# Three idle products ahead of the second small turn, two adaLN tiles summed on VectorE, x's last turns ahead of the sums

## The chip, the core and the metric

The kernel runs on one core of a Trainium2 chip. The core has four engines that compute, each with its own queue, worked off in order: TensorE (PE in the profile; PEld is its loading of weights, which overlaps its products), VectorE (DVE), ScalarE (ACT) and GpSimd (POOL). SyncE (SP) issues transfers between the device's memory (HBM) and the core's own memory. Products are written to PSUM banks, from which DVE and ACT read. The metric is the device time of one execution in microseconds (us), the median of several runs.

## The reference

One layer, float32, on x of 256 tokens by 2048:

```python
h = rmsnorm(x, norm_g)                                   # (256, 2048)
mod = silu(c) @ ada_w + ada_b                            # (1, 3 * 2048)
shift, scale, gate = split(mod, 3)
h = h * (1.0 + scale) + shift
b_gate, c_gate, v, g = split(h @ sc_w_in, 4)             # sc_w_in: 2048 x 4 * 4096
u = causal_depthwise_conv(c_gate * v, conv_w)            # width 3
y = (b_gate * u * silu(g)) @ sc_w_out                    # sc_w_out: 4096 x 2048
out = rmsnorm(x + gate * y, final_g)
```

The large work is two products, h @ sc_w_in and y @ sc_w_out. adaLN's vector-matrix product, silu(c) @ ada_w, reads a matrix of 2048 x 6144.

## The kernel before, in words

Every large product is made of three products in a shorter float format: each operand is split into a rounded part (`hi`) and the remainder (`lo`), and hi\*hi, hi\*lo and lo\*hi are added up. `hi` of a weight tile is made by ACT (`split_hi`, L314), `lo` by DVE (`split_lo`, L319). The transposed and modulated h is split in the same way into the two halves of `hT` (`modulate`, L293).

The model dimension 2048 is cut into 16 blocks `k` of 128 rows. h's block k can be used as soon as adaLN's shift and scale for it are there. adaLN is therefore made in groups of two blocks: the group's columns of ada_w come in as tiles `at`, and the sum over the 16 row blocks, each times its value of silu(c), is built up. For all groups but the first DVE does that alone, on a tile `gv` (`ada_sums`, L420), and four transposes and a `reduce_sum` (`ada_done`, L429) end it. The products h @ sc_w_in start with the blocks that are ready and come back later for the rest: a part (`part`, L469) is one chunk of 512 output columns of one of the four quarters, over the blocks k0 to k1. In the first stage every part covers the first two blocks alone, so it needs one half tile of weights (128 x 1024, `raw_s`), or `raw0` for the very first part; later parts work on whole tiles (128 x 2048). A part's PSUM bank is copied out by ACT (`acc`, L465), added by DVE (L467), or refilled from `acc` ahead of the next products (L477). `plan` (L52) decides the order of parts and adaLN pieces from constants for costs.

Two kinds of order follow one another. From L181 to L379 the instructions are pinned: each engine runs them in the order in which the program writes them (`in_order`). This is the front, which the change touches. Behind it a scheduler orders the instructions of each engine, from its own estimate of time and from priorities; `behind(ended)` keeps chosen ones behind the front's last instruction of their engine. So an edit of the front can also move instructions behind it.

The front, engine by engine:

- SP issues the four pieces of x, twelve pieces of ada_w (`first_ada`, six tiles: rows k = 0 to 3, 4 to 7, 8 to 11, 12 and 13, 14, 15), the two pieces of raw0, and then the transfers behind the front. ACT issues the three small vectors c, norm_g and ada_b.
- PE makes the first small turn (c, L242), the second small turn (norm_g and ada_b, `tp_v`, L245), the idle products (`idle`, L248, whose results nobody reads), the turns of x (`turn_x`, L277, four groups of eight transposes, each group a bank `tp_x` of four blocks), and its share of the first adaLN group's sums (`sum0`, L348).
- The rows k in `ON_PE` are summed on PE, where silu(c), broadcast, is the moving operand and all sums add up in one bank, `sums0`. The other rows are summed on DVE in `gv0`; at the end PE adds `gv0` to the same bank, in two halves (L373). Row k = 15 is divided: its shift half goes to PE, its scale half to DVE.
- DVE squares the second half of the tokens of x, copies the second turn's result to `vec`, makes `rstd`, then runs the sums in gv0, the remainder of raw0's first block (L375), the sum with the bias (`mod`, L297), and the scalings and remainders of h (L301, L304).
- ACT makes silu(c), squares the first half of the tokens, scales the four pieces of x by rstd (L344), copies the turned x to `xs` with the norm's weight (`keep_x`, L286), rounds raw0's two blocks, and makes the rounded part of hT (L300).

A bank for `tp_x` is one of three (tag "mm"), which the parts behind the front use too, so the fourth group waits until ACT has emptied the first. The small turns, the idle products and `sums0` share two banks with the tag "sm".

Of the kernel before, what the change touches and what calls it, by code (L numbers as in the profile page):

```python
# [117 lines left out]
def short_conv_layer(ctx: ExitStack, tc: tile.TileContext, x, c, norm_g, ada_w, ada_b, w_in, conv_w, w_out, final_g, out):  # L118
# [17 lines left out]
    def slot(shape, name, dtype=F32):  # L136
        return slots.tile(shape, dtype, tag="slot", name=name)
# [48 lines left out]
    HX = D // 2  # L186
    GIVE = 300
    LEAD = 80
    IDLE = 6
    ON_PE = (3, 7, 10, 11, 13, 15)  # L190
    xt = [[slot([P, HX], f"x{t}{dh}") for dh in range(2)] for t in range(TT)]
    nc.scalar.dma_start(rows1[64:80, :], c.rearrange("o (k p) -> (o k) p", p=P))
    for t in range(TT):
# [33 lines left out]
    def turn(rows, lo, n, dst):  # L227
        tp = psum.tile([P, 512], F32, tag="sm", name="tp_v", bufs=2)[:, : n - lo]
        nc.tensor.transpose(tp, rows[lo:n, :], ident[lo:n, lo:n])
        if dst is not None:  # L230
            nc.vector.tensor_copy(dst, tp)
        return tp


    def idle(n):
        for _ in range(n):
            nc.tensor.matmul(tp_idle, ident, ones[:, 0:1].to_broadcast([P, 512]), start=True, stop=True)
# [4 lines left out]
    silu = nc.scalar.activation(silu_c, turn(rows1, 64, 80, None), AF.Silu)  # L242
    root = nc.scalar.activation(warm, eps_t, AF.Sqrt)
    tc.add_manual_dep(root.ins, silu.ins.name, after, reason="one change of table")
    tp_v = turn(rows1, 0, 64, None)  # L245
    gT = vec[:, 0:KT]
    bias = vec[:, KT : 3 * KT].rearrange("p (s k) -> p s k", s=2)
    idle(IDLE)  # L248


    ssq = const.tile([P, 2, TT], F32, tag="ssq", name="ssq")
# [25 lines left out]
    def turn_x(j):  # L277

        tp = psum.tile([P, CT, T], F32, tag="mm", name="tp_x")
        for i in range(CT):  # L280
            for t in range(TT):
                c0 = (j * CT + i) % 8 * P
                nc.tensor.transpose(tp[:, i, t * P : (t + 1) * P], xt[t][j // 2][:, c0 : c0 + P], ident)
        return tp

    def keep_x(j, tp):  # L286
        for i in range(CT):
            k = j * CT + i
            nc.scalar.activation(xs[j][:, i], tp[:, i], AF.Copy, scale=gT[:, k : k + 1])
# [3 lines left out]
    def modulate(k0, nk, sums):  # L293

        ks = slice(k0, k0 + nk)
        sums = sums.rearrange("p (s k) -> p s k", s=2)
        nc.vector.tensor_tensor(out=mod[:, :, ks], in0=sums, in1=bias[:, :, ks], op=ALU.add)  # L297
        for k in range(k0, k0 + nk):
            hf = xs[k // CT][:, k % CT, :]
            nc.scalar.activation(hh_[:, k], hf, AF.Identity, bias=mod[:, 0, k : k + 1], scale=mod[:, 1, k : k + 1])  # L300
            nc.vector.tensor_scalar(  # L301
                out=hf, in0=hf, scalar1=mod[:, 1, k : k + 1], scalar2=mod[:, 0, k : k + 1], op0=ALU.mult, op1=ALU.add
            )
            nc.vector.tensor_tensor(out=hl_[:, k], in0=hf, in1=hh_[:, k].bitcast(F32), op=ALU.subtract)  # L304
# [43 lines left out]
    def sum0(k, rows, col, halves=(0, 1)):  # L348


        for o in range(2 * NK0):
            if o // NK0 in halves:
                nc.tensor.matmul(
                    sums0[:, o * P : (o + 1) * P], rows[:, o // NK0, (o % NK0) * P : (o % NK0 + 1) * P],
                    col.to_broadcast([P, P]),
                    start=k == ON_PE[0] and o == 0, stop=k is None, skip_group_check=True,
                )

    for k in range(KT):
        c_k = silu_c[:, k : k + 1]  # L360
        at, gv = first_ada[k], gv0
        if k in ON_PE:
            if k == 10:
                keep_x(2, turn_x(2))
            sum0(k, at, c_k, (0,) if k == KT - 1 else (0, 1))
            if k < KT - 1:
                continue
            at, gv = at[:, 1], gv0[:, 1]
        if k == 0:
            nc.vector.tensor_scalar_mul(gv, at, c_k)  # L370
        else:
            nc.vector.scalar_tensor_tensor(out=gv, in0=at, scalar=c_k, in1=gv, op0=ALU.mult, op1=ALU.add)
# [2 lines left out]
    pieces0 = [split(raw0[:, 0 : CT * P], CT * P)]  # L375
    hi0 = [split_hi(raw0[:, k * CT * P : (k + 1) * CT * P], CT * P) for k in range(1, NK0)]
    modulate(0, NK0, sums0.rearrange("p (o f) -> p o f", o=2 * NK0)[:, :, 0])
    tp_3 = turn_x(3)
    pinned.close()  # L379
    with behind(ended):  # L380
        keep_x(3, tp_3)
# [350 lines left out]
```

## Time and profile before

| | us |
|---|---|
| median of 3 runs | 913.6 |
| lowest and highest run | 913.55, 913.6 |
| span of the profiled execution | 911.9 |
| PE busy | 895.7 |
| DVE busy | 616.2 |
| ACT busy | 464.6 |

The span goes from the first to the last profiled instruction; a run's time also holds what lies around it. A row of a timeline gives start, duration, engine, line, operation, the tiles written and read, their shapes, the count of instructions merged, and in brackets the idle time of the engine before it with what ended it. A row of the chain of waits gives start, duration and what was waited for. A row of the transfers' view gives the count, the size and the time from issue to landing. Matmuls overlap, so a row's busy time is a little longer than the distance to the next.

### The profile page before, as it was taken

The page shows a single profiled execution, that of the slowest core. Times are in us where ns is not written, and L with a number is a line of the kernel's source. Part 1 is how long each engine was busy: PE and PEld are TensorE (multiplying, and loading weights), DVE is VectorE, ACT ScalarE, POOL GpSimd, SP SyncE. Part 2 cuts the span into 40 slices and gives each one's busy share as a digit, 9 for nine tenths or more (in the row PEclk, how much of TensorE's full clock was granted, in tenths as well). Part 3 has the DMA queues.
Part 4 walks back from the last instruction along what each step waited for, and adds up shares of the span by engine and source line. Part 5 has one row for each costly group of instructions (what it writes and reads, how often), then busy time and mean ns, then how long its engine had stood idle before and what let it go on. Part 6 is the DMA issues. An engine that isn't in the chain of part 4 may idle for free.

```text
span 911.9 us, 16239 instructions
## 1 busy us (share of the span) xinstructions
PE 895.7 (98%) x7047; PEld 858.5 (94%) x7047; DVE 616.2 (68%) x593; ACT 464.6 (51%) x413; POOL 0.7 (0%) x6
## 2 busy tenths in 40 slices
PE   6999999999999999999999999999999999999996
PEld 4999999999999999999999999999999988888885
DVE  4889999989888899765545555545554544555882
ACT  6768856665558756743334433444333333443333
POOL 0000000000000000000000000000000000000000
PEclk9999999999999999999999999999999999999998
DMA  9999999999998698676656665566656486655542
GB/s 309 367 371 353 365 325 351 356 369 352 338 328 275 197 359 301 201 246 197 186 188 197 200 201 186 187 195 200 200 188 188 140 331 231 203 201 186 185 139 92
DMA packets 163752, 227.65 MB, mean 250 GB/s; under 512 B 5680, under 2 KB 104160, under 8 KB 163296
## 3 DMA queue, kind: packets, MB, share of 16 engines
q1 hardware_dynamic: 163552, 226.56, 74.8%
q8 instruction: 55, 0.90, 0.4%
q14 instruction: 17, 0.14, 0.0%
q10 hardware_dynamic: 128, 0.04, 0.0%
HBM read 224.49 MB, written 2.10 MB: 248 GB/s over the span
## 4 chain that ended last, share of the span: by engine, by line
PE 94%; DMA 3%; ACT 1%; SPq 1%; DVE 0%; issue 0%; ACTq 0%
PE mm_b L444 38%; PE mm_s L444 36%; PE mm_o L631 6%; PE mm_o L629 6%; PE mm_o L630 6%; DMA raw_s<-in_sc_w_in_dram 2%; DMA at<-in_ada_w_dram 1%; SPq L210 1%; DMA x<-in_x_dram 1%; ACT hi L314 0%; PE ps_gate L568 0%; PE tp_g L434 0%; ACT acc L465 0%; DVE lo L319 0%; ACT hT L300 0%; SPq L413 0%
## 5 line engine op out<-in xcount | busy, mean ns | idle before, releaser
L444 PE MATMUL mm_s<-hT,hi 128*128 128x256 f32 x2048 | 350.5, 277 | 0.2
L444 PE MATMUL mm_b<-hT,hi 128*128 128x256 f32 x2048 | 348.8, 276 | 0.0
L444 PEld LDWEIGHTS mm_s<-hT,hi 128*128 128x128 f32 x2048 | 308.7, 188 | 1.1 <-ACT hT L300 0.4
L444 PEld LDWEIGHTS mm_b<-hT,hi 128*128 128x128 f32 x2048 | 308.7, 188 | 0.2 <-issue 0.2
L444 PE MATMUL mm_b<-hT,lo 128*128 128x256 f32 x1024 | 282.6, 276 | 0.0
L444 PE MATMUL mm_s<-hT,lo 128*128 128x256 f32 x1024 | 282.2, 277 | 0.2 <-DVE lo L319 0.2
L319 DVE TENSOR_TENSOR lo<-raw,hi 128x2048 fp32r<-128x2048 f32 (+1 forms) x66 | 148.0, 2244 | 136.8 <-ACT hi L314 136.8
L314 ACT CAST hi<-raw 128x2048 fp32r<-128x2048 f32 (+1 forms) x66 | 123.7, 1874 | 200.2 <-PE mm_b L444 156.1
L444 PEld LDWEIGHTS mm_b<-hT,lo 128*128 128x128 f32 x1024 | 192.2, 188 | 0.2 <-issue 0.2
L444 PEld LDWEIGHTS mm_s<-hT,lo 128*128 128x128 f32 x1024 | 191.7, 188 | 0.7 <-DVE lo L319 0.6
L319 DVE TENSOR_TENSOR lo<-raw_s,hi 128x2048 fp32r<-128x2048 f32 (+1 forms) x80 | 147.6, 1850 | 25.6 <-ACT hi L314 24.6
L314 ACT CAST hi<-raw_s 128x2048 fp32r<-128x2048 f32 (+1 forms) x80 | 124.2, 1559 | 72.0 <-PE mm_s L444 59.2
L319 DVE TENSOR_TENSOR lo<-raw_o,hi 128x2048 fp32r<-128x2048 f32 x32 | 73.3, 2292 | 66.3 <-ACT hi L314 66.1
L314 ACT CAST hi<-raw_o 128x2048 fp32r<-128x2048 f32 x32 | 61.0, 1907 | 107.2 <-PE mm_o L631 83.7
L630 PE MATMUL mm_o<-lo,y 128*128 128x512 f32 x256 | 99.7, 391 | 0.0
L629 PE MATMUL mm_o<-hi,y 128*128 128x512 f32 x256 | 99.3, 389 | 0.0
L631 PE MATMUL mm_o<-hi,y 128*128 128x512 f32 x256 | 99.3, 389 | 0.0
L427 DVE SCALAR_TENSOR_TENSOR gv<-at,silu_c,gv 128x512 f32<-128x512 f32 x105 | 78.6, 749 | 2.2 <-DMA at<-in_ada_w_dram 0.3
L465 ACT COPY acc<-mm_s 128x1024 f32<-128x1024 f32 x54 | 54.5, 1012 | 35.9 <-PE mm_s L444 35.9
L630 PEld LDWEIGHTS mm_o<-lo,y 128*128 128x128 f32 x256 | 48.1, 188 | 10.2 <-issue 0.2
L631 PEld LDWEIGHTS mm_o<-hi,y 128*128 128x128 f32 x256 | 48.0, 188 | 10.2 <-issue 0.2
L629 PEld LDWEIGHTS mm_o<-hi,y 128*128 128x128 f32 x256 | 48.1, 188 | 9.9
(89 smaller groups left out, 349.6 us busy)
## 6 DMA issues: line engine op xcount, KB each, us to landing
raw<-in_sc_w_in_dram SPq DMA_DIRECT2D x64, 1024.0 KB, 5.7
raw_s<-in_sc_w_in_dram SPq DMA_DIRECT2D x47, 1024.0 KB, 7.9
raw_o<-in_sc_w_out_dram SPq DMA_DIRECT2D x32, 1024.0 KB, 5.1
at<-in_ada_w_dram SPq DMA_DIRECT2D x114, 256.0 KB, 8.0
raw_s<-in_sc_w_in_dram SPq DMA_DIRECT2D x33, 512.0 KB, 7.1
at_g<-in_ada_w_dram SPq DMA_DIRECT2D x32, 512.0 KB, 7.8
at<-in_ada_w_dram SPq DMA_DIRECT2D x6, 512.0 KB, 9.6
x<-in_x_dram SPq DMA_DIRECT2D x4, 512.0 KB, 6.4
```

The costliest lines, as they stand in the source:

```text
L210: nc.sync.dma_start(at[:, :, s, :], adas[:, j : j + kk, s, 0 : NK0 * P])
L314: nc.scalar.copy(hi[:, :n], raw[:, :n])
L319: nc.vector.tensor_tensor(out=lo[:, :n], in0=raw[:, :n], in1=hi[:, :n].bitcast(F32), op=ALU.subtract)
L427: nc.vector.scalar_tensor_tensor(out=gv, in0=at4[:, i], scalar=c_k, in1=gv, op0=ALU.mult, op1=ALU.add)
L444: mm = last_mm[0] = nc.tensor.matmul(dst, w, h[:, k], start=begins and left, stop=ends, skip_group_check=True)
L465: nc.scalar.copy(acc[ch, q], bank)
L629: nc.tensor.matmul(po, yh, hi[:, o], start=opens, stop=False, skip_group_check=True)
L630: nc.tensor.matmul(po, yh, lo[:, o], start=False, stop=False, skip_group_check=True)
L631: nc.tensor.matmul(po, yl, hi[:, o], start=False, stop=ct == NCT - 1, skip_group_check=True)
```

## The change

The six idle products behind the second small turn become three ahead of it and five behind it. Rows k = 3 and k = 7 of the first adaLN group leave `ON_PE`: their eight products on PE go, and DVE's loop over `gv0` gets two more sums. The fourth group of turns of x, which stood behind the closing sums, now follows the third group, ahead of the sums for k = 10; its result is copied out by ACT at the same place in the program as before, behind the front.

```diff
-    IDLE = 6
-    ON_PE = (3, 7, 10, 11, 13, 15)
+    IDLE = (3, 5)
+    ON_PE = (10, 11, 13, 15)
@@
     tc.add_manual_dep(root.ins, silu.ins.name, after, reason="one change of table")
+    idle(IDLE[0])
     tp_v = turn(rows1, 0, 64, None)
     gT = vec[:, 0:KT]
     bias = vec[:, KT : 3 * KT].rearrange("p (s k) -> p s k", s=2)
-    idle(IDLE)
+    idle(IDLE[1])
@@
         if k in ON_PE:
             if k == 10:
                 keep_x(2, turn_x(2))
+                tp_3 = turn_x(3)
             sum0(k, at, c_k, (0,) if k == KT - 1 else (0, 1))
@@
     modulate(0, NK0, sums0.rearrange("p (o f) -> p o f", o=2 * NK0)[:, :, 0])
-    tp_3 = turn_x(3)
     pinned.close()
     with behind(ended):
         keep_x(3, tp_3)
```

The built program also differs behind the front, where the scheduler chooses. The same transfers leave SP, the first 33 in the same order; later ones change places, the first of them a piece of ada_w that now precedes a pair of weight pieces. On DVE and ACT some instructions behind the front change places too, and on PE a few products of neighbouring parts and the transposes of `ada_done`.

## The prediction

> **What bounds the kernel now.** I read the page first, then who waited for whom on TensorE (PE), then the chain of waits in order of time, and last the timeline of the first 65 us.
>
> ```profile
> span 911.9 us, 16239 instructions
> PE 895.7 (98%) x7047; PEld 858.5 (94%) x7047; DVE 616.2 (68%) x593; ACT 464.6 (51%) x413; POOL 0.7 (0%) x6
> ```
>
> ```profile
> PE tp_v L229 <- DMA rows<-in_ada_b_dram: 4.3, 1, 4.3
> ```
>
> PE is busy for 98% of the span. Of the 16 us in which it is not, the largest piece is the wait above, 4.3 ahead of the second small turn. The median of the runs, 913.6, lies 1.7 us above this execution's span of 911.9; I add the same 1.7 to every span below. What moves the end is when PE gets its first products and where it stands still after that. The chain of waits says what holds those points:
>
> ```profile
> 31.06 6.67 DMA raw_s<-in_sc_w_in_dram
> 38.91 1.24 DVE lo L319
> 40.20 15.17 PE mm_s L444 x131
> 55.80 12.15 PE mm_s L444 x107
> 94.97 0.92 ACT mm_s L477
> ```
>
> Columns: start, duration, what. Up to 40.2 us the chain runs over transfers, not over PE: the fifth half tile of weights leaves at 31.06, lands at 37.73, is rounded, its remainder taken, and PE goes on at 40.20. From there on it is PE, at 12.15/107 = 0.114 us a product, with one break before 95.9 where it waits for a bank that ScalarE (ACT) refills. So time won ahead of 40.2 is worth nothing unless that half tile comes earlier, and time lost before it is absorbed as far as PE stands waiting there.
>
> ```profile
> 8.81 7.07 PE L237 MATMUL tp_idle<-ones,ident 128*128 128x512 f32 x12
> 10.68 0.34 PEld L237 LDWEIGHTS tp_idle<-ones,ident 128*128 128x128 f32 x1 [0.52 <-issue]
> 12.28 0.19 PEld L237 LDWEIGHTS tp_idle<-ones,ident 128*128 128x128 f32 x1 [0.41 <-issue]
> 12.66 4.27 ACT L344 ACTIVATE x<-x,rstd 128x1024 f32<-128x1024 f32 x4 [0.23 <-DVE rstd L268]
> 15.73 1.91 PE L283 MATMUL tp_x<-ident,x 128*128 128x128 f32 x16
> 16.49 2.33 DVE L372 SCALAR_TENSOR_TENSOR gv<-at,silu_c,gv 128x512 f32<-128x512 f32 x3 [1.04 <-DMA at<-in_ada_w_dram]
> 17.90 1.83 SPq L177 DMA_DIRECT2D raw<-in_sc_w_in_dram  x2
> 19.51 3.63 DVE L372 SCALAR_TENSOR_TENSOR gv<-at,silu_c,gv 128x512 f32<-128x512 f32 x5 [0.69 <-DMA at<-in_ada_w_dram]
> raw<-in_sc_w_in_dram SPq DMA_DIRECT2D x1, 256.0 KB, 5.2
> 23.16 1.34 ACT L314 CAST hi<-raw 128x512 fp32r<-128x512 f32 x2 [1.26 <-DVE gv L372]
> 23.26 1.05 PE L353 MATMUL sum<-ones,gv 128*128 128x128 f32 x8
> 23.81 0.69 DVE L319 TENSOR_TENSOR lo<-raw,hi 128x512 fp32r<-128x512 f32 x1 [0.67 <-ACT hi L314]
> 24.15 1.03 PE L283 MATMUL tp_x<-ident,x 128*128 128x128 f32 x8
> 24.42 0.15 DVE L297 TENSOR_TENSOR mod<-sum,vec 128x4 f32<-128x4 f32 x1
> 24.67 1.09 ACT L300 ACTIVATE hT<-xs,mod 128x256 fp32r<-128x256 f32 x2 [0.17 <-DVE mod L297]
> 25.32 0.72 PE L444 MATMUL mm_s<-hT,hi 128*128 128x256 f32 x4
> ```
>
> Columns: start, duration, engine, line; the one raw row is of the transfers' view and ends in us to landing. The last link before PE's first real product at 25.32: raw0 (issued 17.90, the first of its two pieces 5.2 under way, so landed at 23.1) is rounded by ACT at 23.16, VectorE (DVE) takes the remainder from 23.81, and the sum mod, next in DVE's order, starts at 24.42 as that remainder ends. PE's own last sums end at 23.26+1.05 = 24.31. Both chains meet at 24.4; the one through raw0 hangs on a transfer.
>
> **The change part by part.**
>
> *Idle products.* Six become eight, three of them ahead of the second small turn. Two records make one product. While the clock is low (a load beside them takes 0.34, from 12.28 on 0.19) four records take 12.28-8.81 = 3.47, 0.87 each; the other eight, to 8.81+7.07 = 15.88, 0.45 each. Before, the block began behind the second turn, whose rows land 4.3 us after the first turn, at 8.5. Now three products run from the first turn's end, about 4.2: to 9.4 if all six records are slow, to 8.6 if the clock rises 3.47 after their start as it did here. So the second turn slips by 0 to 0.9. Only a copy waits for it, which stands on DVE behind two squares of x: nothing. Five more products take 4.5 and end between 13.4 and 14.3. The first turns need ACT's first two scalings of x (12.66+4.27/2 = 14.8), so they start at 14.8 instead of 15.73, where the idle products held them.
>
> *x's last turns.* 8 transposes (1.03 us) leave the place at 24.15 and follow the third group. They need the last scaling (16.9) and the bank that ACT's first four keeps free (16.8+1.55, the length of four in the row under (a)): they end at 19.3, before the tile of the sums for k = 10 lands at 19.39. PE loses nothing there, and the work they hid behind at 24.15, the wait for hT, now shows as 1.4 us of idle PE.
>
> *Two tiles from PE to DVE.* PE loses 16 records of 0.112. DVE gains two sums of 2.33/3 = 0.78. They fall into the bracketed 1.04 and 0.69 of waiting for transfers: the first tile's sums end 0.78 later, still before 16.49, the second's at 16.49+4x0.787 = 19.64 instead of 19.51, so the chain ends 0.13 later, at 23.27. PE's closing sums now start on the first half at 22.8 and end at 23.9, 0.4 earlier. That 0.4 is worth nothing: mod stands behind the remainder of raw0, which stands behind a landing that does not move, since the order of the first 33 transfers is unchanged. First product: 25.32, as before.
>
> *What the scheduler does behind the front.* The built order shows three displacements, and these carry the sum.
>
> (a) ACT's four keeps for the last turns now stand ahead of the rounding of the first half tile, and DVE's first sum of the next adaLN group ahead of its remainder.
>
> ```profile
> 26.61 1.55 ACT L289 ACTIVATE xs<-tp_x,vec 128x256 f32<-128x256 f32 x4
> 27.48 1.22 DVE L319 TENSOR_TENSOR lo<-raw_s,hi 128x1024 fp32r<-128x1024 f32 x1
> 28.62 0.48 DVE L425 TENSOR_SCALAR gv<-at,silu_c 128x512 f32<-128x512 f32 x1
> 21.84 0.47 SPq L413
> at<-in_ada_w_dram SPq DMA_DIRECT2D x1, 256.0 KB, 6.1
> 39.56 0.39 PE L444 MATMUL mm_s<-hT,hi 128*128 128x256 f32 x2
> ```
>
> That sum needs a transfer issued at 21.84 and 6.1 under way: 27.93. It runs from 28.03 to 28.5, then the remainder for 1.22 to 29.72, where before it ended at 28.70. PE, which went on as that came, now goes on at 29.77. Before that it does two products of the second half tile, which the new order puts there. From 29.77 there are 92 products to the fifth half tile: 29.77+92x0.114+0.1 = 40.3. Before, PE reached that tile at 39.56 and stood until 40.20, then lost 0.1 at the restart. What is left of 0.7 us of delay behind that point is 0.2.
>
> (b) Where the second adaLN group is done, the remainder of the first whole tile moves behind the making of hT, and on ACT hT moves behind a copy of a finished part.
>
> ```profile
> 57.83 1.09 ACT L300 ACTIVATE hT<-xs,mod 128x256 fp32r<-128x256 f32 x2
> 57.96 2.29 DVE L319 TENSOR_TENSOR lo<-raw_s,hi 128x2048 fp32r<-128x2048 f32 x1
> 58.83 2.02 ACT L465 COPY acc<-mm_s 128x1024 f32<-128x1024 f32 x2
> 60.83 0.73 DVE L301 TENSOR_SCALAR xs<-xs,mod 128x256 f32<-128x256 f32 x2
> 61.48 0.76 DVE L304 TENSOR_TENSOR hT<-xs,hT 128x256 fp32r<-128x256 f32 x2
> 56.91 0.39 PE L444 MATMUL mm_s<-hT,hi 128*128 128x256 f32 x2
> 62.57 0.28 PE L444 MATMUL mm_s<-hT,lo 128*128 128x256 f32 x1
> ```
>
> Before, the remainder ended at 60.25, 2.3 us ahead of the product that reads it (62.57). Now: the part whose last products precede 56.91 ends at 57.1+0.25 with the 0.2 of (a); its copy takes ACT until 58.26; the first hT comes at 58.86; DVE makes the two pairs, each scaling waiting for its own hT (1.14 to where the next can start: 0.42, 0.43 and 0.29, near half of each row's two), with a sum (0.70), the last subtraction (0.33) and a second sum (0.69) between, each as from one start to the next: 58.89+2.86 = 61.75; the remainder 2.29, to 64.04. PE wants it at 62.8: a stall of 1.3, and 0.1 at the restart, so 1.4. Bounds: nothing, if the copy and the pairs run ahead of this reckoning by its own 1.3; 2.3 (the whole length of a whole tile's remainder), if one more transfer comes late. I take 1.4, where the two reckonings from rows meet: the order puts about 3.7 us more DVE work ahead of this remainder (two scalings, two subtractions, three sums) against 2.3 of slack, which leaves 1.4 too.
>
> (c) The wait ahead of 95.94 (a bank refilled until 94.97+0.92) came from two parts run interleaved on PE. The new order runs them one after the other, and the refill is some 4 us ahead of its use: 0.3 won back, with the restart.
>
> Sum: 0 + 0.2 + 1.4 - 0.3 = 1.3; span 913.2, time 914.9.
>
> **The rivals.**
>
> *The order is harmless.* The DVE finds its gaps elsewhere, (b) costs nothing, (a) and (c) stand: 913.6+0.2-0.3 = 913.5. For it: 1.3 rests on a reckoning over some ten instructions. Against it: the copy cannot start before PE ends that part.
>
> *The clock falls in the new gap (slower).* PE idles from 23.9 to 25.3 and shorter before. If that is enough, the stretch of low clock measured here, 3.5 us at half rate, comes again at 25.3 and costs half of it, 1.7: 916.6. It decides as soon as products after 25.3 start 0.23 apart. No row here shows PE idle for less than 4 us, so the bounds are 0 and 1.7; I take 0, as the gap is a third of the shortest idle stretch ahead of a low clock. The Trainium skill ("TensorE: Matmul & The Clock Gate", section "What's actually happening") has the clock fall after an idle window of about 3.4 us; by that rule the term is 0 too, and it speaks against fearing the gap. Its 3.4 us of activity before the clock rises agree with the 3.5 above.
>
> *A second stall near 331 us (slower).*
>
> ```profile
> 298.95 2.29 DVE L319 TENSOR_TENSOR lo<-raw_s,hi 128x2048 fp32r<-128x2048 f32 x1 [2.95 <-ACT hi L314]
> 325.19 2.29 DVE L319 TENSOR_TENSOR lo<-raw_s,hi 128x2048 fp32r<-128x2048 f32 x1 [0.89 <-ACT hi L314]
> 331.54 0.28 PE L444 MATMUL mm_s<-hT,lo 128*128 128x256 f32 x1
> ```
>
> Seven more gate sums (5.2 us at 0.75) stand ahead of the remainder that now ends at 327.48, 4.1 us ahead of its product. If none finds a gap, PE waits 5.2-4.1 = 1.1 there: 914.9+1.1 = 916.0. Against it: DVE's wait of 2.95 before 298.95 alone takes the excess. It decides if the sums' transfers come too late for that gap.
>
> **How the numbers follow.** Forecast 914.9: 0.50. Harmless order: 0.21. Stall near 331: 0.19. Clock: 0.08. Something that wins over 0.2%: 0.02, since all stalls after 25.3 together are under 1.1 us. 0.2%, about what a measurement here can tell from no change, is 1.8 us: 911.8 to 915.4. The forecast spreads by its term (b), and an eighth of its chance lies above 915.4. Slower: 0.19+0.08+0.06 = 0.33; faster: 0.02, rounded up to 0.03; same: 0.64. Range 913.1 to 916.7: it leaves out a third of the harmless case, half of the clock's, and the tails beyond the bounds of (b). The forecast's own range is 914.2 to 915.6.
>
> **What would show it.** Right: first product at 25.3; a wait for lo near 29.7; PE's fifth half tile at 40.3 without a wait; a wait for lo of about 1.3 us at 62.8; none before 95.9 plus 1.6. Wrong: a first product at or before 25.0, products 0.23 apart after it, no wait at 62.8, or a wait past 100 us.

## The result, and the profile after

| | before | after |
|---|---|---|
| median of 21 runs each, us | 913.76 | 914.85 |
| ratio, 95% interval | 1 | 1.0014 (1.0008 to 1.0021) |
| span of the profiled execution, us | 911.9 | 912.8 |

The change costs 1.1 us. The ratio of the runs says 0.14%, with an interval that lies wholly above 1: a small loss, but clear of the noise, within the 0.2% that the prediction counts as no change, and 0.05 us from its number. (Lines of the changed kernel are one or two higher than before's: L320 is L319 of before, L445 is L444. In the experiments they shift by some more.)

Who waited for whom on TensorE, after (in all, times, longest):

```profile
PE mm_s L445 <- ACT hT L301: 1.2, 1, 1.2
PE mm_s L445 <- DVE lo L320: 1.2, 2, 1.0
```

The timeline after, from the front to the last place where the two kernels differ in a wait:

```profile
4.24 5.35 PE L237 MATMUL tp_idle<-ones,ident 128*128 128x512 f32 x6
9.53 0.27 PE L229 MATMUL tp_v<-ident,rows 64*128 64x64 f32 x1
...
14.14 0.27 PE L284 MATMUL tp_x<-ident,x 128*128 128x128 f32 x1
...
18.20 1.09 PE L284 MATMUL tp_x<-ident,x 128*128 128x128 f32 x8 [0.46 <-ACT xs L290]
...
22.60 1.23 PE L354 MATMUL sum<-ones,gv 128*128 128x128 f32 x8
25.06 0.74 PE L445 MATMUL mm_s<-hT,hi 128*128 128x256 f32 x4 [1.23 <-ACT hT L301]
...
27.70 0.49 DVE L426 TENSOR_SCALAR gv<-at,silu_c 128x512 f32<-128x512 f32 x1 [0.40 <-DMA at<-in_ada_w_dram]
28.10 1.22 DVE L320 TENSOR_TENSOR lo<-raw_s,hi 128x1024 fp32r<-128x1024 f32 x1
29.37 0.39 PE L445 MATMUL mm_s<-hT,lo 128*128 128x256 f32 x1
...
40.15 0.28 PE L445 MATMUL mm_s<-hT,lo 128*128 128x256 f32 x1
...
56.93 1.02 ACT L466 COPY acc<-mm_s 128x1024 f32<-128x1024 f32 x1 [1.96 <-PE mm_s L445]
57.84 1.09 ACT L301 ACTIVATE hT<-xs,mod 128x256 fp32r<-128x256 f32 x2
58.84 1.90 ACT L315 CAST hi<-raw_s 128x2048 fp32r<-128x2048 f32 x1
59.59 0.75 DVE L428 SCALAR_TENSOR_TENSOR gv<-at,silu_c,gv 128x512 f32<-128x512 f32 x1
60.59 0.75 DVE L428 SCALAR_TENSOR_TENSOR gv<-at,silu_c,gv 128x512 f32<-128x512 f32 x1
61.25 2.29 DVE L320 TENSOR_TENSOR lo<-raw_s,hi 128x2048 fp32r<-128x2048 f32 x1
62.17 0.39 PE L445 MATMUL mm_s<-hT,hi 128*128 128x256 f32 x2
63.59 0.39 PE L445 MATMUL mm_s<-hT,lo 128*128 128x256 f32 x1 [1.03 <-DVE lo L320]
...
91.50 1.01 ACT L478 COPY mm_s<-acc 128x1024 f32<-128x1024 f32 x1
...
95.16 1.01 ACT L478 COPY mm_s<-acc 128x1024 f32<-128x1024 f32 x1
```

What to see, in order of time:

- The first product starts at 25.06 instead of 25.32. The transfers from SyncE lie some 0.25 us earlier in this execution (raw0 leaves at 17.68 and lands at 22.80, before at 17.90 and 23.07). That is chance: over the profiles of this document raw0 leaves anywhere from 17.49 to 17.99. Against its transfers the front ends where it did.
- Between the first product and 31.6 us PE falls back by 0.64, counted product by product: from 0.27 ahead of the kernel before to 0.37 behind it. At 40.15 it takes the remainder of the fifth half tile without a stop; before it stood until 40.20, a stop worth 0.53, so that from there on it is 0.17 ahead again.
- The one new stop: the product at 62.17 is followed by one at 63.59 that waited 1.03 for the first whole tile's remainder. ScalarE copies a finished part, makes both hT and only then rounds that tile (58.84 to 60.74); VectorE puts two sums between, and the remainder runs from 61.25 to 63.54. With the restart the stop is worth 1.3: products from there on start 1.14 later than before, those ahead of it 0.17 earlier. In the kernel before that rounding stood ahead of both hT (57.83):

```profile
56.01 1.92 ACT L314 CAST hi<-raw_s 128x2048 fp32r<-128x2048 f32 x1 [0.81 <-DMA raw_s<-in_sc_w_in_dram]
```

- No break near 96: the two refills end at 92.51 and 96.17, ahead of parts that PE opens at 94.03 and 99.47. Behind that place the changed kernel is 0.79 behind the kernel before, and 0.9 at PE's last product.

### The profile page after: what moved, and what is told of

It reads as the page before. It is cut to its first block, busy times and chain, and to the rows that moved or that the text cites. A ratio compares the mean times of both kernels' runs of the same rounds, so it can differ in the third digit from the quotient of the medians.

```text
span 912.8 us, 16223 instructions
## 1 busy us (share of the span) xinstructions
PE 897.9 (98%) x7035; PEld 857.7 (94%) x7035; DVE 616.0 (67%) x595; ACT 464.5 (51%) x413; POOL 0.7 (0%) x6
## 4 chain that ended last, share of the span: by engine, by line
PE 95%; DMA 2%; ACT 1%; SPq 1%; DVE 1%; issue 0%; ACTq 0%
PE mm_b L445 38%; PE mm_s L445 37%; PE mm_o L632 6%; PE mm_o L631 6%; PE mm_o L630 6%; DMA at<-in_ada_w_dram 1%; SPq L210 1%; DMA x<-in_x_dram 1%; DMA raw_s<-in_sc_w_in_dram 1%; PE ps_gate L569 0%; PE tp_g L435 0%; DVE lo L320 0%; ACT hi L315 0%; ACT xs L290 0%; DVE gv L428 0%
## 5 line engine op out<-in xcount | busy, mean ns | idle before, releaser
L445 PE MATMUL mm_s<-hT,hi 128*128 128x256 f32 x2048 | 350.6, 277 | 1.3 <-ACT hT L301 1.2
L445 PE MATMUL mm_b<-hT,hi 128*128 128x256 f32 x2048 | 348.8, 276 | 0.0
L445 PEld LDWEIGHTS mm_s<-hT,hi 128*128 128x128 f32 x2048 | 308.7, 188 | 2.2 <-ACT hT L301 1.4
L445 PEld LDWEIGHTS mm_b<-hT,hi 128*128 128x128 f32 x2048 | 308.4, 188 | 0.2 <-issue 0.2
L445 PE MATMUL mm_s<-hT,lo 128*128 128x256 f32 x1024 | 282.2, 277 | 1.2 <-DVE lo L320 1.2
L445 PE MATMUL mm_b<-hT,lo 128*128 128x256 f32 x1024 | 282.6, 276 | 0.0
L320 DVE TENSOR_TENSOR lo<-raw,hi 128x2048 fp32r<-128x2048 f32 (+1 forms) x66 | 148.1, 2244 | 138.1 <-ACT hi L315 138.1
L445 PEld LDWEIGHTS mm_s<-hT,lo 128*128 128x128 f32 x1024 | 191.7, 188 | 1.8 <-DVE lo L320 1.8
L445 PEld LDWEIGHTS mm_b<-hT,lo 128*128 128x128 f32 x1024 | 192.2, 188 | 0.2 <-issue 0.2
L320 DVE TENSOR_TENSOR lo<-raw_s,hi 128x2048 fp32r<-128x2048 f32 (+1 forms) x80 | 147.3, 1849 | 21.9 <-ACT hi L315 21.7
L315 ACT CAST hi<-raw_s 128x2048 fp32r<-128x2048 f32 (+1 forms) x80 | 124.1, 1558 | 55.9 <-PE mm_s L445 29.2
L320 DVE TENSOR_TENSOR lo<-raw_o,hi 128x2048 fp32r<-128x2048 f32 x32 | 73.3, 2291 | 66.0 <-ACT hi L315 66.0
L631 PEld LDWEIGHTS mm_o<-lo,y 128*128 128x128 f32 x256 | 48.1, 188 | 10.2 <-issue 0.2
```

Source lines behind the costliest of these rows:

```text
L315: nc.scalar.copy(hi[:, :n], raw[:, :n])
L320: nc.vector.tensor_tensor(out=lo[:, :n], in0=raw[:, :n], in1=hi[:, :n].bitcast(F32), op=ALU.subtract)
L445: mm = last_mm[0] = nc.tensor.matmul(dst, w, h[:, k], start=begins and left, stop=ends, skip_group_check=True)
L631: nc.tensor.matmul(po, yh, lo[:, o], start=False, stop=False, skip_group_check=True)
```

## The experiments

Twelve kernels, each timed against the kernel before on the same chip; that one took 913.67, 913.82 and 913.70 in the three sets of runs, so small differences between the medians of different sets say little, and the ratio is what to compare. First the whole set; "first product" and the waits (us, the longest of that place) are read from one profile of each, as in the timeline above. Waits between 27 and 32 us are not in the table: turns_alone has one of 0.55 there and no_moved_sums one of 0.99, the others none over 0.3.

| run | what differs | first product | wait for lo at 62 to 65 | wait for a refill at 95 to 96 | median | ratio, 95% interval |
|---|---|---|---|---|---|---|
| (changed kernel) | | 25.06 | 1.0 | none | 914.85 | 1.0014 (1.0008 to 1.0021) |
| round_first | change, rounding ahead of hT | 25.19 | none | none | 914.22 | 1.0005 (0.9996 to 1.0014) |
| sums_behind | change, two sums behind the remainder | 25.09 | 0.6 | 1.2 | 915.72 | 1.0023 (1.0014 to 1.0032) |
| swap_in_before | before, rounding behind hT | 26.49 | 0.6 | 1.0 | 915.36 | 1.0019 (1.0010 to 1.0028) |
| idle_alone | before + new idle products | 25.05 | none | none | 913.59 | 0.9998 (0.9989 to 1.0007) |
| sums_alone | before + moved sums | 25.10 | none | none | 913.22 | 0.9993 (0.9984 to 1.0002) |
| turns_alone | before + moved turns | 26.30 | none | none | 915.17 | 1.0016 (1.0007 to 1.0025) |
| no_new_idle | change - idle products | 26.03 | 1.0 | 1.2 | 916.52 | 1.0031 (1.0019 to 1.0042) |
| no_moved_sums | change - moved sums | 25.17 | 1.0 | 1.2 | 917.11 | 1.0036 (1.0023 to 1.0048) |
| no_late_turns | change - moved turns | 25.19 | none | none | 913.22 | 0.9997 (0.9988 to 1.0005) |
| gap_of_3 | change, other tiles on PE | 26.04 | none | 1.0 | 915.91 | 1.0028 (1.0017 to 1.0040) |
| gap_of_6 | change, two tiles on PE | 28.42 | none | none | 917.63 | 1.0048 (1.0034 to 1.0061) |
| no_idle_at_all | change, no idle products | 25.77 | none | 1.2 | 915.57 | 1.0021 (1.0012 to 1.0031) |

### Is the stop at 62 us the loss, and which engine's order makes it?

**round_first** adds two links behind the front of the changed kernel (`made[k]` is the instruction that makes hT of block k, `rounded` the rounding of the first whole tile):

```diff
+            if (ch, q, s0) == (3, 2, 0):
+                for k in (2, 3):
+                    tc.add_manual_dep(made[k].ins, rounded[3, 2, 0].ins.name, after, reason="in order")
```

> The changed front kept whole; one link added: on ScalarE the two hT of the second adaLN group stand behind the rounding of the first whole tile, which also puts that tile's remainder ahead of hT on VectorE, as before the change. Theory (the stall of 1.3 us at 62 us, made by the order, is the whole loss, and the front itself costs 0.2 at most): no wait for lo at 62 us, first product at 25.1 to 25.3 as in the changed kernel, 914.85 - 1.3 = 913.5 us, so 0.9997 of before, 0.9990 to 1.0003. Rival (the new front costs the time, by the gap on TensorE or a later start, and the order is harmless): the wait goes but the time stays at 914.9, 1.0012. A wait of up to 0.8 for the third whole tile's remainder near 74 us, ahead of which the order puts 1.5 us more VectorE work against 0.7 us of slack before, would make it 914.3.

The timeline of round_first at the place:

```profile
57.93 1.91 ACT L319 CAST hi<-raw_s 128x2048 fp32r<-128x2048 f32 x1
59.74 1.09 ACT L303 ACTIVATE hT<-xs,mod 128x256 fp32r<-128x256 f32 x2
...
59.88 2.29 DVE L324 TENSOR_TENSOR lo<-raw_s,hi 128x2048 fp32r<-128x2048 f32 x1 [0.35 <-ACT hi L319]
```

The remainder ends at 62.17 and PE wants it at 62.49: no stop. PE's last product ends at 904.27, 0.20 ahead of before's (904.47) and 1.10 ahead of the changed kernel's (905.37), which is the theory to a tenth. The median gives back only half: it lies 0.55 above the kernel before of its own set, where the changed kernel lies 1.1 above. The two ratios' intervals overlap, so by the times alone the gain is likely and not settled. In the profile what follows PE's last product took 8.0 instead of 7.4 us: the last of the eight output transfers was 1.0 in issuing instead of 0.4, and landed at 911.16 instead of 910.77, though PE had ended earlier. Why is open (three of its eleven runs took 913.7). So the stop at 62 us is shown to be what PE loses; that the whole of the 1.1 in the median is this stop is not shown.

**sums_behind** moves VectorE's two sums behind the remainder and leaves ScalarE as it was (`taken` is the remainder of the first whole tile):

```diff
+        if (k0, j) == (4, 2):
+            for i in (2, 3):
+                tc.add_manual_dep(gv_sums[4, i].ins, taken[3, 2, 0].ins.name, after, reason="in order")
```

> The changed kernel with VectorE's two sums of the next adaLN group (0.75 us each) moved behind the remainder of the first whole tile; ScalarE's order stays as changed, with the copy and both hT ahead of that tile's rounding. Theory (ScalarE's order holds the remainder: its rounding ends at 60.74 whatever VectorE does): the remainder starts at 60.8 and ends at 63.05 instead of 63.54, PE waits 0.7 instead of 1.2, 914.85 - 0.5 = 914.35 us, 1.0006. Rival (VectorE's work ahead of the remainder decides, as the prediction reckoned): it starts at 60.0, ends at 62.3, no wait, 913.5 us, 0.9997.

The timeline of sums_behind, at 59 us and at 92:

```profile
59.00 1.90 ACT L315 CAST hi<-raw_s 128x2048 fp32r<-128x2048 f32 x1
...
59.87 0.43 DVE L305 TENSOR_TENSOR hT<-xs,hT 128x256 fp32r<-128x256 f32 x1
60.93 2.29 DVE L320 TENSOR_TENSOR lo<-raw_s,hi 128x2048 fp32r<-128x2048 f32 x1 [0.64 <-ACT hi L315]
...
92.16 1.91 ACT L315 CAST hi<-raw_s 128x2048 fp32r<-128x2048 f32 x1
93.97 1.96 ACT L488 COPY mm_s<-acc 128x1024 f32<-128x1024 f32 x2
...
95.04 0.50 PE L455 MATMUL mm_s<-hT,hi 128*128 128x256 f32 x2 [1.17 <-ACT mm_s L488]
```

VectorE is free at 60.3 and stands for 0.64 until the rounding is done: ScalarE's order holds the remainder, as the theory has it, and the rival falls. The wait shrinks from 1.03 to 0.6, as expected. But the time rises: the order built for this kernel puts the next whole tile's rounding (92.16) ahead of both refills, and PE waits 1.17 for a bank at 95.04. With its restart that stop is worth 1.4, and 915.72 less 1.4 is 914.3, near the 914.35 expected without it. A stop of the kind that the change had removed has come back through ScalarE's order.

**swap_in_before** gives the kernel before, with its own front, ScalarE's changed order (`copied` is the copy of the finished part):

```diff
+            if (ch, q, s0) == (3, 2, 0):
+                for k in (2, 3):
+                    tc.add_manual_dep(made[k].ins, copied[2, 3].ins.name, after, reason="in order")
+                    tc.add_manual_dep(rounded[3, 2, 0].ins, made[k].ins.name, after, reason="in order")
```

> The kernel before with its own front; only ScalarE's order at the end of the second adaLN group is set as in the changed kernel: the copy of a finished part, then both hT, then the first whole tile's rounding. VectorE's order follows: hT ahead of that tile's remainder. Near 95 us the order built for it puts a whole tile's rounding ahead of the first refill, and no parts are interleaved. Theory (the loss is the order, whatever the front): first product at 25.2 and the wait at 40.2 as before; copy to 58.1, hT to 59.2, rounding to 61.0, remainder to 63.3 against 62.5 wanted: a wait of 0.8 to 1.0 at 62 us; a wait of 0.4 to 1.4 for the refill near 94 us; 913.8 - 0.3 + 1.2 to 2.4 = 914.7 to 915.9, 1.001 to 1.0023. Rival (it takes the new front): 913.8, 1.0000.

915.36, in the range given. Its timeline:

```profile
59.62 1.90 ACT L318 CAST hi<-raw_s 128x2048 fp32r<-128x2048 f32 x1
...
61.55 2.29 DVE L323 TENSOR_TENSOR lo<-raw_s,hi 128x2048 fp32r<-128x2048 f32 x1 [0.72 <-ACT hi L318]
63.90 0.39 PE L448 MATMUL mm_s<-hT,lo 128*128 128x256 f32 x1 [0.56 <-DVE lo L323]
...
95.49 0.50 PE L448 MATMUL mm_s<-hT,hi 128*128 128x256 f32 x2 [0.99 <-ACT mm_s L483]
```

Again the remainder waits for the rounding and PE for the remainder, 0.6 where 0.8 to 1.0 was expected, and 1.0 for a refill at 95.49. The same stops come with the old front, so they do not need the new one. One thing was not expected: the first product came at 26.49, because of the clock (last section); of that delay of 1.2, 0.6 was left behind 40 us. So the time agrees with the theory, but it is the two stops in the trace that show it.

### The parts, alone and left out

**idle_alone** is the kernel before with the two calls of `idle` as in the change:

```diff
-    IDLE = 6
+    IDLE = (3, 5)
```

> Only the idle products changed: three ahead of the second small turn, five behind it; nothing else. Theory: built with the first whole tile's rounding and remainder ahead of hT and with a refill ahead of the whole tile's rounding near 93 us, so no wait at 62 or 95 us: 913.4 us, 0.9997. Rival (idle products ahead of a small turn cost their 1.0 us): 914.7, 1.001.

913.59: nothing lost, none of the waits. The rival falls.

**sums_alone**:

```diff
-    ON_PE = (3, 7, 10, 11, 13, 15)
+    ON_PE = (10, 11, 13, 15)
```

> Only the two tiles of sums moved from TensorE to VectorE. Theory: rounding and remainder of the first whole tile stand ahead of hT, a refill ahead of the whole tile's rounding near 93 us, x's last turns still behind the sums: no wait at 62 or 95 us, 913.4 us, 0.9997. Rival (1.56 us more on VectorE ahead of the first remainder delays the first product): the first product 0.8 to 1.5 later than 25.2, of which 0.3 to 1.0 is left past 40 us: 914.0 to 914.8.

913.22, first product 25.10: two more sums on VectorE delay nothing. The rival falls.

**turns_alone**:

```diff
                 keep_x(2, turn_x(2))
+                tp_3 = turn_x(3)
@@
-    tp_3 = turn_x(3)
     pinned.close()
```

> Only x's last turns moved ahead of the sums. Theory: rounding and remainder of the first whole tile ahead of hT, so no wait at 62 us; near 95 us the first refill comes early, the second stands behind two roundings of whole tiles: 913.4 us, 0.9997, if the second of these lands by 95 us as in the changed kernel, a wait of up to 1.1 and 914.5, 1.0008, if it lands at 96.3 as before the change. Rival (the turns ahead of the sums are what cost the 1.1 us): 914.9, 1.0012, with no wait at 95 us, and the loss already there at 62 us.

915.17: here the theory fell. As the rival has it, there is no wait at 62 or 95, and the loss is there before 62 us. It is not the changed kernel's loss, though, whose first product is in place. The timeline of turns_alone:

```profile
15.89 1.91 PE L283 MATMUL tp_x<-ident,x 128*128 128x128 f32 x16
17.63 1.95 PE L353 MATMUL sum<-silu_c,at 128*128 128x128 f32 x16
19.42 1.91 PE L283 MATMUL tp_x<-ident,x 128*128 128x128 f32 x16
21.16 3.29 PE L353 MATMUL sum<-silu_c,at 128*128 128x128 f32 x28
24.30 1.05 PE L353 MATMUL sum<-ones,gv 128*128 128x128 f32 x8
25.39 0.16 DVE L297 TENSOR_TENSOR mod<-sum,vec 128x4 f32<-128x4 f32 x1 [1.04 <-PE sum L353]
26.30 0.74 PE L444 MATMUL mm_s<-hT,hi 128*128 128x256 f32 x4 [0.95 <-ACT hT L300]
...
29.90 1.22 DVE L319 TENSOR_TENSOR lo<-raw_s,hi 128x1024 fp32r<-128x1024 f32 x1
31.17 0.39 PE L444 MATMUL mm_s<-hT,lo 128*128 128x256 f32 x1 [0.55 <-DVE lo L319]
```

PE is busy without a gap from 15.89 to 25.35, and the sum mod waits for it: with the first 16 records of sums still on PE and the turns starting 1.75 later than in the changed kernel, the eight moved turns push the closing sums from 22.60 to 24.30 and the first product to 26.30. That is about half of the delay. The other half comes behind the front: VectorE runs two sums of the next group ahead of the first half tile's remainder (29.90), and PE waits 0.55 for it at 31.17. From 31.6 us on PE is 2.2 later than before; the former stop at 40 and the former break at 95.9 take some 0.9 of that, and 1.35 is left at its last product.

**no_new_idle** is the change with `IDLE = (0, 6)`.

> The change without its edit of the idle products: six stand behind the second small turn, none ahead. The order built for it has the first whole tile's rounding and remainder behind hT, as in the changed kernel. Theory (the order decides): a wait for lo of 1.0 to 1.3 us at 62 us, 914.9 us, 1.0012; up to 1.0 more if the 2.3 us of further VectorE work that this order puts ahead of the remainder near 152 us (slack 1.26 there in the changed kernel) finds no gap. Rival (the parts add): less than the change, 914.2 to 914.6. Rival (the idle products are what costs): 913.8.

916.52: above the range. The wait at 64 (1.0) came as expected; two things were not in the expectation: the first product at 26.03, and a wait for a refill at 96. The timeline of no_new_idle:

```profile
8.98 8.46 PE L237 MATMUL tp_idle<-ones,ident 128*128 128x512 f32 x12
17.28 3.79 PE L284 MATMUL tp_x<-ident,x 128*128 128x128 f32 x32
...
93.23 1.92 ACT L315 CAST hi<-raw_s 128x2048 fp32r<-128x2048 f32 x1
95.03 1.97 ACT L478 COPY mm_s<-acc 128x1024 f32<-128x1024 f32 x2
```

Idle products that start at 8.98 hold x's turns until 17.28, 3.1 later than in the changed kernel, and the moved turns make that the front's end. In this profile the clock rose late, 6.1 us into the idle products (last section); in the profile of the kernel before, where it rose after 3.5, the turns started at 15.73. At 93.23 a rounding stands ahead of both refills, as in sums_behind.

**no_moved_sums** is the change with the six tiles left in `ON_PE`.

> The change without its edit of the sums: six tiles stay on TensorE; idle products and x's last turns as changed. Theory (only what the order does to ScalarE near 60 and 95 us is dear): built with both hT ahead of the first whole tile's rounding, so a wait of 1.0 to 1.3 for lo at 62 us, and with a whole tile's rounding ahead of both refills near 93 us, as in the two runs that waited 1.3 there, so a second wait of 1.2 to 1.4 for a bank: 914.85 + 1.3 = 916.2 us, 1.0027. Rival (the parts add up, each with a price in the front): less than the changed kernel, 914.2 to 914.6, 1.0005 to 1.0009.

917.11: both waits as the theory has them, and 1.0 more at 30.5. The timeline of no_moved_sums there:

```profile
28.82 0.49 DVE L426 TENSOR_SCALAR gv<-at,silu_c 128x512 f32<-128x512 f32 x1 [1.40 <-DMA at<-in_ada_w_dram]
...
30.49 0.39 PE L445 MATMUL mm_s<-hT,lo 128*128 128x256 f32 x1 [0.99 <-DVE lo L320]
```

VectorE's first sum of the next group, ahead of a remainder in this order, waited 1.40 for its transfer; in the changed kernel it waited 0.40 and ran at 27.70. The first product is in place, at 25.17, with all six tiles on TensorE and the turns moved.

**no_late_turns** is the change with `tp_3 = turn_x(3)` put back behind `modulate`.

> The change without the move of x's last turns, which stay behind the sums; idle products and the two tiles of sums as changed. The order built for it has the first whole tile's rounding ahead of both hT on ScalarE and its remainder ahead of hT on VectorE. Theory (the order decides): no wait at 62 us, no break at 96 us, 913.5 us, 0.9997. Rival (the parts add, each with a price of its own in the front; the turns are one of three): a part of the 1.1 us is left, 914.2 to 914.6, 1.0005 to 1.0009.

913.22, ratio 0.9997: no wait at 62 or 95. Together with sums_alone it is the fastest of the set; whether either beats the kernel before is not settled (both intervals reach over 1).

So the parts do not add up. Where the rounding of the first whole tile stands behind hT (the change, no_new_idle, no_moved_sums, sums_behind, and swap_in_before, where it was put there) there is the wait at 62 to 65; where the next one stands ahead of the refills (no_new_idle, no_moved_sums, sums_behind, swap_in_before, gap_of_3, no_idle_at_all) there is the wait at 95; where neither holds and the front is in time (idle_alone, sums_alone, no_late_turns), the kernel takes 913.2 to 913.6 (914.2 in round_first, with its longer tail).

### The gap on TensorE, and its clock

**gap_of_3** and **gap_of_6** lengthen PE's idle stretch ahead of the first products by moving tiles of the sums:

```diff
-    ON_PE = (10, 11, 13, 15)
+    ON_PE = (3, 7, 10, 11)
```

and `ON_PE = (3, 7)`, with the late turns then at k = 3.

> The changed front with TensorE's four tiles of sums at k = 3, 7, 10, 11 in place of 10, 11, 13, 15, so that TensorE idles from about 21.2 until VectorE's chain, 1.0 longer, ends at 24.1; a gap of 2.9 us instead of 1.5. The order built for it has neither the wait at 62 nor that at 95 us. Theory (a gap of this length leaves the clock alone): closing sums at 24.1, first product at 26.0, products 0.114 apart, 0.8 of the delay left past 40 us: 914.3. Rival (the clock falls in the gap): products 0.23 apart for some 3 to 6 us after it, 915.7 to 917.5.

> The changed front with only the tiles k = 3 and 7 on TensorE; the turns follow k = 3's place, and TensorE idles from about 20 until VectorE's chain, two more sums of 0.78 longer, ends at 25.7: 5.7 us. Theory (an idle stretch of this length lowers the clock): closing sums and products 0.23 apart for 2.7 to 6.1 us, the range in which the clock rose in the runs so far, so 1.4 to 3.0 on top of a first product 2.4 later: 917 to 919. Rival (the clock stays): products 0.114 apart at once, 915.5 to 916.

Busy time by stretch, gap_of_3 (the column after POOL's is the granted clock):

```profile
22.00:24.00 2.00, 0.07 (x1) 0.07 (x1) 1.93 (x4) 1.13 (x2) 0.00 (x0) 1.00 1.04 386
24.00:26.00 2.00, 1.09 (x8) 0.90 (x8) 0.64 (x2) 0.71 (x3) 0.00 (x0) 0.91 1.06 370
26.00:28.00 2.00, 1.96 (x9) 1.96 (x10) 1.91 (x5) 2.00 (x6) 0.00 (x0) 0.50 1.09 376
28.00:30.00 2.00, 2.00 (x15) 2.00 (x15) 1.96 (x4) 2.00 (x3) 0.00 (x0) 0.74 1.05 365
```

and its closing sums and first products:

```profile
23.93 1.16 PE L354 MATMUL sum<-ones,gv 128*128 128x128 f32 x8 [2.17 <-DVE gv L374]
26.04 1.23 PE L445 MATMUL mm_s<-hT,hi 128*128 128x256 f32 x4 [0.95 <-ACT hT L301]
```

The clock fell: products start 0.21 apart until 29.1, and the four that take 0.74 in all in the changed kernel take 1.23. So the theory of gap_of_3 fell, and its rival was right that the clock falls: PE had stood for 2.17 and 0.95, with eight sums between. But the price that the rival put on it did not come. Further on in gap_of_3:

```profile
29.38 2.35 DVE L320 TENSOR_TENSOR lo<-raw_s,hi 128x1024 fp32r<-128x1024 f32 x2
30.73 0.31 PE L445 MATMUL mm_s<-hT,lo 128*128 128x256 f32 x1
```

This order has two sums of the next group ahead of the first half tile's remainder, VectorE is busy without a gap from 26.02 on, and the remainder, the first of the two in the row, ends at 30.60. PE takes it at 30.73. On a full clock PE would have been there by about 29.2 (an estimate: 28 products of 0.114 behind 26.04) and stood until 30.6, so the clock cost about 0.1. Of the 1.7 that PE was late by at 39 us its former wait at 40 took 0.56. The 1.0 at 95 was not expected either: this order has a rounding ahead of both refills, which the expectation misread. The 915.91 lies in the rival's range, but through VectorE's order and the refill.

In gap_of_6 PE stood for 4.5; the clock fell 0.6 us after its sums went on (0.62 granted between 26 and 28) and rose at 33.3. There it cost 1.0: the first half tile's remainder ended at 32.98, and PE came to it only at 34.02. 917.63 is within the theory's range, with a smaller part of the clock than the 1.4 to 3.0 reckoned. In the changed kernel the granted clock is 1.00 in every one of these stretches, with a gap of 1.23. (The column shows a fall, but not the low clock at the start of a run: it reads 1.00 there too, where the idle products take twice as long. The rise is read from their lengths.)

**no_idle_at_all** has `IDLE = (0, 0)`.

> The changed kernel without any idle products. x's first turns open at 14.2 to 14.5 on a low clock, 0.23 apart instead of 0.11, until 2.7 to 6.1 us after that. Theory (the idle products are what lets the turns precede the sums): the last turn ends at 20.5 to 22 instead of 19.3, the sums behind it end 1 to 2 later, first product 25.6 to 26.8; the order built for it has no wait at 62 us but a whole tile's rounding ahead of both refills near 93 us, a wait of 1.3: 915.0 to 916.5. Rival (the idle products do nothing here): first product 25.1, 914.7.

All of the theory came: the turns run 0.21 apart until 19.9, the first product starts at 25.77, PE waits 1.2 for the refill, 915.57. The rival falls.

## Why the prediction was right, and where not

- **Idle products, first term 0: right here, for a narrower reason than given.** The second turn slipped by 1.0 (reckoned 0 to 0.9) and nothing waited for it. But the price of nothing holds only for the whole change. Two pairs differ in this edit alone: the changed kernel and no_new_idle (first product 25.06 and 26.03), no_moved_sums and turns_alone (25.17 and 26.30). With the turns moved, the earlier idle products are what keeps the first product at 25; the lighter PE is not needed for it. In no_new_idle a late rise of the clock has a part in the 1.0.
- **x's last turns: "PE loses nothing there" is true of the change** (turns end at 19.3 as reckoned, first product in place) and false of the edit by itself, with which the first product comes 1.0 later.
- **Two tiles to VectorE: right.** The closing sums end at 23.8 (reckoned 23.9), and sums_alone confirms that VectorE's chain has the room.
- **(a), +0.2: right in kind, about +0.1 measured.** The remainder ended at 29.32, PE fell back by 0.64 (reckoned 0.7), and the former stop at 40 gave 0.53 back. idle_alone has ScalarE's half of the new order only, VectorE's remainder still ahead of the sum: PE fell back by 0.43 there, and the stop at 40 took it all. The price was less certain than stated: in no_moved_sums the same sum's transfer landed 1.1 later, and 1.0 was lost.
- **(b), +1.4: 1.3 measured, in the right place; its mechanism half right.** The prediction let VectorE's work ahead of the remainder set its start, which it does in the changed kernel (61.25, reckoned 61.75), and took the meeting of its "two reckonings from rows" as agreement. It overlooked that ScalarE's rounding of that tile had itself moved behind hT. By the prediction's account the wait would go with VectorE's two sums. sums_behind shows that 0.4 of it goes and 0.6 is left, which is the rounding; round_first and swap_in_before take the stop away and bring it back with ScalarE's order.
- **(c), -0.3: 0.35 measured**, with the refill 1.5 and 3.3 us ahead of its use rather than 4. The other side of it was not seen: in half of the variants a refill comes too late by a whole us.
- **The rivals.** The harmless order fell with the wait at 63.59. No stall came near 331: PE never waits for a tile of weights behind 63.6 in the changed kernel. The clock did not fall, but the reason given ("the gap is a third of the shortest idle stretch ahead of a low clock") was a poor bound: in gap_of_3 it fell with a longest stop of 2.2. The 1.7 reckoned as its price is not borne out: about 0.1 in gap_of_3, where VectorE was the later one, and 1.0 in gap_of_6.
- **What bounds the kernel.** The 4.3 ahead of the second small turn is not PE's largest idle piece: 7.4 us pass between its last product and the end of the span. No term rests on it.

The sum by the trace: 0.1 + 1.3 - 0.35 = 1.05, less 0.25 for transfers that happened to run earlier in this execution: 0.8, against 0.9 between the spans and 1.1 between the medians. That the number is met to 0.05 is in part luck: a loss of 1.3 was forecast and 1.1 came, and the kernel before took 913.76 in these runs, not the 913.6 to which the 1.3 was added.

## What to carry to other kernels

Read the built order on every engine behind an edit, not only where the edit is: a front that ended where it did before cost some 1 us forty us later, mainly because a rounding moved behind two small instructions on ScalarE. For a late operand follow it back over each engine that makes it (rounding, then remainder), and take the latest, not the longest queue. And do not price edits of a front one by one: two of the three are free, and the third is dear alone. Beside the new idle products it leaves the first product in place, and yet no_late_turns, the change without it, takes 913.22: what it costs then is the order that is built around it. And a slow stretch on one engine costs only as much as it outlasts what the others make it wait for: look for the next operand that it meets.

## What the runs showed of the hardware

At the start of a run the clock's rise takes anything between 3 and 6 us of work. The twelve idle records of before (8.81 to 15.73) and those of no_new_idle (8.98 to 17.28) are the same work; at 0.85 a slow and 0.43 a fast one, four were slow in the one and seven in the other: 3.5 against 6.1 us. In sums_behind the clock rose after some 3.0, within the six records ahead of the second turn:

```profile
4.27 4.30 PE L237 MATMUL tp_idle<-ones,ident 128*128 128x512 f32 x6
```

where the changed kernel took 5.35 for them. A late rise is what made the first product of swap_in_before late (turns from 16.95, 1.2 after before's). Of the five profiles whose idle products start at 8.7 to 9.0, three have the turns at 16.7 to 17.3 and two at 15.7 to 15.9. That is what idle products that start at 4.1 to 4.5 guard against: their late rises end by 10.2, and x's turns start between 13.6 and 14.6 in every run that has them.

The clock falls on less than one long stop, too: 2.17 and 0.95 us with 1.2 of work between were enough (the clock fell 0.5 us into the second stop), one stop of 1.23 was not. It then stayed low for 3.4 us in gap_of_3 and for 6.8 in gap_of_6. The Trainium skill ("TensorE: Matmul & The Clock Gate", section "What's actually happening") describes a free-running window of about 3.4 us and says that the moment of the rise varies with it, by half a us either way; it has the clock fall after an idle window of that length. The runs agree that the rise varies, but here by 3.1 us; and the fall did not need an idle stretch of 3.4.
